# Down projection of a hybrid decoder layer: 8 of 22 feature blocks of each half as two Strassen steps of seven products, with a plain tile behind each unit

## The chip, the cores and the metric

The kernel runs on one core of a Trainium2 chip, in one launch. The metric is the device time of one execution in microseconds (us). Three executions of the kernel before took 1077.84, 1078.82 and 1079.95 us; their median is 1078.82 us. The profile is of one further execution, which took 1077.04 us.

## The reference, cut to what matters

One decoder layer on 256 tokens (S) and a model width of 2048 (D). The matrices are float32.

```python
h = rmsnorm(x, attn_norm_g)
proj = h @ w_in                       # one combined input projection
o_mla = mla_group(...)                # 8 heads, latent queries and keys
o_nsa = nsa_group(...)                # 16 heads, three branches
x = x + concatenate([o_mla, o_nsa]) @ w_o
h = rmsnorm(x, ffn_norm_g)
x = x + (silu(h @ w_gate) * (h @ w_up)) @ w_down     # D_FF = 5632
return rmsnorm(x, final_norm_g)
```

The change is about the product with `w_down`, a matrix of 5632 x 2048. Its left factor has 256 rows (the tokens) and 5632 columns (the features), which are 44 blocks of 128.

## The kernel before

The layer is worked through in stages: input projection, attention, output projection, and the feed-forward part. The feed-forward part runs in two halves of 22 feature blocks each (NFH = 22). A half first computes the gate and up projections of its 22 blocks, then adds its share of the down projection to `x`. So the order of the long stages is gate and up of half 0, down of half 0, gate and up of half 1, down of half 1, and a short tail with the final norm and the output.

All weights come through one class, `Stream`. The order of the tiles is the list that `program()` returns (from L81 on for this part). A weight tile is 128 x 1024 float32, 512 KB, and is loaded by a DMA that SyncE issues (L122). ScalarE then makes the high part by a cast to the reduced type fp32r (`whi`, L143), and VectorE the low part by subtracting the high part from the raw tile (`wlo`, L145). Each of the three tags (`wraw`, `whi`, `wlo`) has three buffers. A load is issued up to three tiles ahead (DMA_AHEAD, L104), and a split is recorded two tiles ahead (SPLIT_AHEAD, L105). The activations are kept in a high and a low part as well (`aT`), and every product is the sum of three matmuls: high by high, high by low and low by high (L859 to L861).

The down projection of a half goes through four groups of 512 output columns (`dg`, L844), and in each group through 11 tiles of two feature blocks (L864). A tile makes 12 matmuls of 128x128 by 128x512: two halves of the tokens (t), two blocks, three matmuls each. The sums of a group stand in two PSUM banks; behind the 11 tiles VectorE adds them to `x` (L876). In half 1, ScalarE also sums the squares (L880) and GpSimd multiplies by the final gain `gfin` (L882). In the last group the matmuls of four tiles for the second half of the tokens are held back to the end (`held`, L867), and the last tiles' parts have buffers of their own (`W.apart`, L812). The gain is loaded ahead of the gate and up projections, on GpSimd's queue (L811).

The order of TensorE's instructions is the order in which the code records them. The order on the other engines is set by a scheduler from its own model of their times. At the very start, the input projection's first two tiles (880 columns) are each loaded and split in two pieces, cut at column 368 (L111).

Of the kernel before, what the change touches and what calls it, by code (L numbers as in the profile page):

```python
# [9 lines left out]
F32 = mybir.dt.float32  # L10
# [6 lines left out]
P = 128  # L17
# [13 lines left out]
NSA_SCALE = 0.125  # L31


def program():
# [46 lines left out]
    for h in range(2):  # L81
# [6 lines left out]
        s += [("w", ("down", h, dg, j)) for dg in range(4) for j in range(NFH // 2)]  # L88
    return s


def plan():

    return [k[1] for k in program() if k[0] == "w"]
# [6 lines left out]
class Stream:  # L101
# [3 lines left out]
    SPLIT_AHEAD = 2  # L105

    def __init__(self, nc, pool, order, src):
        self.nc, self.pool, self.order, self.src = nc, pool, order, src
        self.raw, self.done = {}, {}
        self.nd = self.ns = self.nu = 0  # L110
        self.cuts = {0: (0, 368, G1W), 1: (0, 368, G1W)}  # L111
        self.apart = {}
        self.share = 0

    def _dma(self, upto):
        while self.nd < min(upto, len(self.order)):
            i = self.nd
            w = width(self.order[i])
            t = self.pool.tile([P, 1024], F32, tag="wraw", name=f"wraw{i}", bufs=self.DMA_AHEAD)
# [3 lines left out]
            self.raw[i] = t  # L123
            self.nd += 1

    def _split(self, upto):
        nc = self.nc
        while self.ns < min(upto, len(self.order)):
            i = self.ns
            self._dma(i + 1)  # L130
            raw = self.raw.pop(i)
            if self.order[i][0] in ("w1k", "w1v"):
                self.done[i] = raw
            else:
                w = width(self.order[i])
                if i in self.apart:
                    hi, lo = (self.apart[i].tile([P, 1024], F32R, name=f"w{n}{i}") for n in ("hi", "lo"))
                else:
                    hi, lo = (self.pool.tile([P, 1024], F32R, tag=f"w{n}", name=f"w{n}{i}", bufs=3)
                              for n in ("hi", "lo"))  # L140
                cut = self.cuts.get(i, (0, w))
# [9 lines left out]
    def get(self, key):  # L151
        i = self.nu
        assert self.order[i] == key, (self.order[i], key)
# [7 lines left out]
def layer_kernel(ctx: ExitStack, tc: tile.TileContext, a: dict, out: bass.AP):  # L161
# [9 lines left out]
    W = Stream(nc, wp, order, wsrc)  # L171
# [22 lines left out]
    oT = cp.tile([P, 16, 2, S], F32R, name="oT")  # L194
# [35 lines left out]
    ap = att.enter_context(tc.tile_pool(name="att", bufs=1))  # L230

# [553 lines left out]
    def gate_up(key, w):  # L785
        n, f, j = key
        hi, lo = w
        if j == 0:
            st[n, f] = bank("ds" if n == "gate" else "PT", f"{n}{f}")
# [19 lines left out]
    aT = fp.tile([P, NFH, 2, S], F32R, name="aT")  # L809
# [4 lines left out]
    def next_weights(*key):  # L814
        assert next(steps) == ("w", key)
        return W.get(key)

    def activate(h, f):

        t2 = fp.tile([P, 2, S], F32, tag="t2", name=f"t2_{h}_{f}", bufs=2)  # L820
        u = fp.tile([P, 2, S], F32, tag="gu", name=f"u_{h}_{f}", bufs=2)
# [7 lines left out]
        nc.vector.tensor_mul(u[:, 1, :], sl, u[:, 1, :])  # L829
        split(aT[:, f, 0, :], aT[:, f, 1, :], u[:, 1, :])  # L830

    for h in range(2):
# [11 lines left out]
        for dg in range(4):  # L844
            if dg % 2 == 0:
                dn = bank2(f"dn{h}_{dg}")
                pts = [dn[:, 0, :], dn[:, 1, :]]
            else:
                pts = [bank("S0", f"dn{h}_{dg}_0"), bank("O", f"dn{h}_{dg}_1")]
            last = h == 1 and dg == 3  # L850
            ntile = NFH // 2

            def down(t, j, w):
                hi, lo = w
# [16 lines left out]
            for t in range(2):  # L871
                if t == 1:
                    for j, w in held:
                        down(1, j, w)
# [148 lines left out]
```

## Time and profile before

| | us |
|---|---|
| three runs | 1077.84, 1078.82, 1079.95 |
| the profiled execution | 1077.04 |
| its span | 1075.3 |
| gate and up, from the last part of half 0 to its end | to 581.2 |
| down projection of half 0 | 581.2 to 700.8 |
| gate and up of half 1 | 700.8 to 946 |
| down projection of half 1 | 946.1 to 1066.9 |
| tail | 1066.9 to 1075.3 |

The span is the stretch between the first and the last instruction that the profiler saw; the execution's own time is 1.74 us more. PE is the matrix engine and PEld its weight loads, DVE is VectorE, ACT is ScalarE, POOL is GpSimd, and SP is SyncE, which issues the loads. A matmul's row is longer than the distance to the next one, since they are pipelined. In a row of the timeline the bracket at the end says how long the engine was idle before the row, and what it was released by. Durations of single matmuls, casts and subtracts are read from the groups by line; the distance of two instructions from their starts.

### The profile page before, as it was taken

The numbers are of one execution on the slowest core, as the hardware profiler recorded it, in microseconds if no ns is written. First come the engines' busy times: TensorE is split into PE (matmuls) and PEld (weight loads), VectorE is DVE, ScalarE is ACT, GpSimd is POOL, SyncE is SP. The second block draws the span as 40 slices with busy tenths as digits, with TensorE's granted clock in tenths as the row PEclk, the third lists the DMA queues.
The fourth block names the chain that finished last, engine by engine and source line by source line (L and its number), as shares of the span: only waits on it lengthen the run. The fifth ranks groups of instructions, "written<-read, shape, count | busy, mean of one in ns | idle before, by whom it ended". The sixth has DMA issues, their size and how long they took to land.

```text
span 1075.3 us, 16205 instructions
## 1 busy us (share of the span) xinstructions
PE 1052.0 (98%) x6102; PEld 920.3 (86%) x6102; DVE 645.7 (60%) x1017; ACT 562.9 (52%) x994; POOL 205.5 (19%) x207
## 2 busy tenths in 40 slices
PE   8999998999999999999999999999999999999996
PEld 7999997888888888888888888888888888888885
DVE  5668889885656555555555444455555555555554
ACT  5748887854455544545444333345445454444442
POOL 2235445533342101011010000001010110101110
PEclk9999999999999999999999999999999999999998
DMA  8845433334456555555555555555556565666653
GB/s 291 277 145 177 134 119 99 103 100 152 135 178 215 183 190 195 183 190 191 185 192 189 192 191 194 193 196 186 188 194 187 186 194 185 191 194 195 192 191 128
DMA packets 54831, 193.57 MB, mean 180 GB/s; under 512 B 6436, under 2 KB 6948, under 8 KB 54624
## 3 DMA queue, kind: packets, MB, share of 16 engines
q1 hardware_dynamic: 54288, 191.36, 54.7%
q8 instruction: 48, 0.79, 0.3%
q0 software_dynamic: 464, 1.17, 0.3%
q14 instruction: 31, 0.25, 0.1%
HBM read 190.41 MB, written 2.10 MB: 179 GB/s over the span
## 4 chain that ended last, share of the span: by engine, by line
PE 88%; DVE 4%; DMA 4%; ACT 2%; issue 1%; SPq 0%; POOL 0%; DVEq 0%; POOLq 0%; ACTq 0%
PE up L794 15%; PE gate L794 15%; PE up L797 8%; PE gate L797 8%; PE dn L860 7%; PE dn L861 7%; PE dn L859 7%; DMA wraw<-in_g_dram 2%; PE ps_q L214 1%; PE woM L743 1%; PE woM L745 1%; PE woM L744 1%; PE ps_q L215 1%; PE ps_q L216 1%; DVE wlo L145 1%
## 5 line engine op out<-in xcount | busy, mean ns | idle before, releaser
L145 DVE TENSOR_TENSOR wlo<-wraw,whi 128x1024 fp32r<-128x1024 f32 (+3 forms) x352 | 417.6, 1187 | 381.0 <-ACT whi L143 379.7
L143 ACT CAST whi<-wraw 128x1024 fp32r<-128x1024 f32 (+2 forms) x352 | 366.4, 1041 | 441.5 <-PE dn L861 127.9
L794 PE MATMUL gate<-h2T,whi 128*128 128x512 f32 x704 | 221.2, 396 | 0.0
L794 PE MATMUL up<-h2T,whi 128*128 128x512 f32 x704 | 221.1, 395 | 0.0
L827 POOL TENSOR_TENSOR u<-t,RB 128x512 f32<-128x512 f32 x44 | 57.2, 1300 | 553.9 <-DVE t L826 553.9
L797 PEld LDWEIGHTS up<-h2T,wlo 128*128 128x128 f32 x704 | 132.2, 188 | 31.3
L797 PEld LDWEIGHTS gate<-h2T,wlo 128*128 128x128 f32 x704 | 132.2, 188 | 31.2
L797 PE MATMUL gate<-h2T,wlo 128*128 128x256 f32 x704 | 138.3, 278 | 0.0
L797 PE MATMUL up<-h2T,wlo 128*128 128x256 f32 x704 | 138.3, 278 | 0.0
L860 PE MATMUL dn<-wlo,aT 128*128 128x512 f32 x352 | 137.1, 389 | 0.6 <-DVE wlo L145 0.6
L859 PE MATMUL dn<-whi,aT 128*128 128x512 f32 x352 | 136.9, 389 | 0.0
L861 PE MATMUL dn<-whi,aT 128*128 128x512 f32 x352 | 136.9, 389 | 0.0
L147 POOL TENSOR_TENSOR wlo<-wraw,whi 128x256 fp32r<-128x256 f32 x70 | 88.5, 1265 | 139.6 <-ACT whi L143 121.1
L794 PEld LDWEIGHTS gate<-h2T,whi 128*128 128x128 f32 x704 | 107.3, 189 | 0.2
L794 PEld LDWEIGHTS up<-h2T,whi 128*128 128x128 f32 x704 | 107.2, 189 | 0.0
L860 PEld LDWEIGHTS dn<-wlo,aT 128*128 128x128 f32 x352 | 66.1, 188 | 14.7 <-DVE wlo L145 1.0
L859 PEld LDWEIGHTS dn<-whi,aT 128*128 128x128 f32 x352 | 66.1, 188 | 13.8
L861 PEld LDWEIGHTS dn<-whi,aT 128*128 128x128 f32 x352 | 66.1, 188 | 13.5
L214 PE MATMUL ps_q<-hT,whi 128*128 128x256 f32 x128 | 37.4, 292 | 1.6 <-ACT RB L210 1.6
L216 PE MATMUL ps_q<-hT,wlo 128*128 128x256 f32 x128 | 36.2, 283 | 0.0
L215 PE MATMUL ps_q<-hT,whi 128*128 128x256 f32 x128 | 36.2, 283 | 0.0
L743 PE MATMUL woN<-whi,oT 128*128 128x512 f32 x64 | 26.6, 416 | 0.4 <-ACT oT L547 0.4
(323 smaller groups left out, 1486.6 us busy)
## 6 DMA issues: line engine op xcount, KB each, us to landing
wraw<-in_w_dram SPq DMA_DIRECT2D x338, 512.0 KB, 3.5
wraw<-in_g_dram SPq DMA_DIRECT2D x14, 440.0 KB, 5.0
x<-in_x_dram SPq DMA_DIRECT2D x4, 512.0 KB, 6.8
out_dram<-x SPq DMA_DIRECT2D x8, 256.0 KB, 2.6
xt<-in_xT_dram SPq DMA_DIRECT2D x3, 512.0 KB, 5.0
gfin<-in_gfin_dram POOLq DMA_DIRECT2D x1, 1024.0 KB, 6.0
wraw<-in_g_dram SPq DMA_DIRECT2D x2, 256.0 KB, 4.1
wraw<-in_g_dram SPq DMA_DIRECT2D x2, 184.0 KB, 3.3
```

The source lines that it names most:

```text
L143: nc.scalar.copy(hi[:, c0:c1], raw[:, c0:c1])
L145: nc.vector.tensor_sub(lo[:, c0:c2], raw[:, c0:c2], hi[:, c0:c2].bitcast(F32))
L147: nc.gpsimd.tensor_sub(lo[:, c2:c1], raw[:, c2:c1], hi[:, c2:c1].bitcast(F32))
L214: nc.tensor.matmul(ps, hi, act[:, 0, :], start=start, stop=False)
L215: nc.tensor.matmul(ps, hi, act[:, 1, :], start=False, stop=False)
L216: nc.tensor.matmul(ps, lo, act[:, 0, :], start=False, stop=stop)
L794: nc.tensor.matmul(pt, hi[:, kk * P:(kk + 1) * P], h2T[:, k], start=k == 0, stop=False)
L797: nc.tensor.matmul(pt[:, 0:S], lo[:, kk * P:(kk + 1) * P], h2T[:, k, 0, :], start=False, stop=k == KD - 1)
L827: nc.gpsimd.tensor_mul(u, t2, RB[:, None, :].to_broadcast([P, 2, S]))
L859: nc.tensor.matmul(pts[t], h_, wh, start=f == 0, stop=False)
L860: nc.tensor.matmul(pts[t], h_, wl, start=False, stop=False)
L861: nc.tensor.matmul(pts[t], l_, wh, start=False, stop=f == NFH - 1)
```

## The change

Take a 2 x 2 block product: the left factor has the blocks A11, A12 (first half of the tokens; first and second feature block) and A21, A22 (second half), the weights B11, B12 (first feature block; first and second group of columns) and B21, B22. Done plainly it is eight block products. In the form of Strassen and Winograd it is seven, with sums of the blocks ahead and sums of the results behind. The change does the first 8 of the 22 feature blocks of each half in this way.

- *Passes, steps and units.* The four groups of columns become two passes of two groups (`p`). A pass has two steps (NS) of four feature blocks; a step has seven units, in the order B11, P1, P3, P2, B22, P4, B21. Each unit is one tile of weights and one product of 6 matmuls. Behind the first six units of step 0 and the first five of step 1 stands a plain tile (12 matmuls); three plain tiles follow at the end. A pass thus has 14 units, 11 + 3 plain tiles, and 22 loads.
- *Sums of weights.* P1 = B11 + B12, P3 = B12 + B22, P2 = P1 + B22 and P4 = P2 + B21 are made by VectorE, in raw float32, from raw tiles; the split follows as for any tile. They take buffers of the tag `wraw`, three of them. A unit's sums are recorded up to four units ahead (SUM_AHEAD), its split two ahead as before.
- *Raw tiles.* From the first down projection on the raw tiles have six buffers of their own (`raw`), and loads run up to six ahead. A buffer is free when the sums and the split that read it are done.
- *Activations.* For the 8 blocks, seven forms of each pair of blocks are kept in two parts (`aS`): A11, A12, A22 and four sums S1 to S4, made by VectorE in `activate` behind every second block of a pair. The other 14 blocks stay as they were (`aN`).
- *Results.* The products and the plain tiles add up in eight PSUM banks per pass. Behind the last product, `combine()` makes the sums: one copy on ScalarE, four operations on VectorE, and four additions to `x` on GpSimd. VectorE adds the four banks of the plain tiles to `x` at the end of the pass.
- *Around it.* The final gain is loaded when the second down projection is recorded, into a buffer of the attention part that is free by then. The second tile of the input projection is loaded and split in one piece. The buffers of `W.apart` are gone, and three tiles are held back in the last pass in place of four. In half 1 gate's banks alternate between the tags S0 and O.

```diff
+NS = 2
+UNITS = ("B11", "P1", "P3", "P2", "B22", "P4", "B21")
+LOADS = {"B11": (0, 0), "P1": (0, 1), "P3": (1, 1), "P4": (1, 0)}
+SUMS = {"P1": ("B11", "B12"), "P3": ("B12", "B22"), "P2": ("P1", "B22"), "P4": ("P2", "B21")}
+RAW_OF = {"B11": "B11", "P1": "B12", "P3": "B22", "P4": "B21"}
+PLAIN = (2, 4), (3, 8)
+PRODUCT = {"B11": (A11, 1), "P1": (S1, 5), "P3": (S3, 7), "P2": (S2, 6), "B22": (S4, 3), "P4": (A22, 4), "B21": (A12, 2)}
+def down_units(h, p):
+    plain = [("w", ("down", h, 2 * p + c, j)) for j in range(2 * NS, NFH // 2) for c in range(2)]
+    s = []
+    for i in range(NS):
+        for u in UNITS:
+            s.append(("sw", u, h, p, i))
+            if u in UNITS[:6 if i < NS - 1 else 5]:
+                s.append(plain.pop(0))
+    return s + plain
...
-        s += [("w", ("down", h, dg, j)) for dg in range(4) for j in range(NFH // 2)]
+        s += [u for p in range(2) for u in down_units(h, p)]
...
     DMA_AHEAD = 3
     SPLIT_AHEAD = 2
+    SUM_AHEAD = 4
...
-        self.cuts = {0: (0, 368, G1W), 1: (0, 368, G1W)}
-        self.apart = {}
+        self.cuts = {0: (0, 368, G1W)}
+        self.raws = (pool, "wraw", 3)
...
+    def _sum(self, upto):
+        while self.na < min(upto, len(self.units)):
+            u = self.units[self.na]
+            if u[0] != "sw":
+                self.parts[self.na] = self._take()
+            else:
+                what, at = u[1], u[2:]
+                if what in RAW_OF:
+                    r = RAW_OF[what]
+                    self.parts[at, r, "i"], self.parts[at, r] = self._take()
+                if what in SUMS:
+                    x, y = (self.parts[at, n] for n in SUMS[what])
+                    t = self.parts[at, what] = self.pool.tile([P, 1024], F32, tag="wraw", name=f"{what}_{self.na}", bufs=3)
+                    self.nc.vector.tensor_add(t, x, y)
+                    if what == "P3":
+                        self._spent(at, "B12")
+                self.parts[self.na] = None, self.parts[at, what]
+            self.na += 1
...
-        self._dma(i + self.DMA_AHEAD)
+        self._dma(self.nr + self.DMA_AHEAD)
+        self._sum(i + (self.SUM_AHEAD if unit[0] == "sw" else self.SPLIT_AHEAD))
         self._split(i + self.SPLIT_AHEAD)
...
-    gfin = fp.tile([P, D], F32, name="gfin")
-    nc.gpsimd.dma_start(gfin, a["gfin"])
-    W.apart = {len(order) - 2: fp, len(order) - 1: fp}
+    aN = fp.tile([P, NN, 2, S], F32R, name="aN")
+    aS = fp.tile([P, NS, 2, 2, 7, P], F32R, name="aS")
+    W.raws = (fp, "raw", 6)
...
+        nc.vector.tensor_sub(s1, a22, a21)
+        nc.vector.tensor_sub(s3, a11, a21)
+        nc.vector.tensor_add(s2, a11, s1)
+        nc.vector.tensor_sub(s4, a12, s2)
...
+        W.DMA_AHEAD = 6
+        if h == 1:
+            gfin = hp.tile([P, D], F32, tag="big", name="gfin")
+            nc.gpsimd.dma_start(gfin, a["gfin"])
+        for p in range(2):
...
+            def combine():
+                e, u, v, w = (temp(f"e{n}_{h}{p}") for n in range(4))
+                nc.scalar.copy(e, m[1])
+                nc.gpsimd.tensor_add(x11, x11, e)
+                nc.vector.tensor_sub(u, e, m[6])
+                nc.vector.tensor_add(w, u, m[5])
+                nc.gpsimd.tensor_sub(x12, x12, w)
+                nc.vector.tensor_add(u, u, m[7])
+                nc.vector.tensor_add(v, u, m[5])
+                nc.gpsimd.tensor_add(x21, x21, u)
+                nc.gpsimd.tensor_sub(x22, x22, v)
...
+            for n, unit in enumerate(todo):
+                w = W.get(unit[1] if unit[0] == "w" else unit)
+                if unit[0] == "sw":
+                    form, to = PRODUCT[unit[1]]
+                    i = unit[4]
+                    mms(to, w, lambda k: [aS[:, i, k, b, form, :] for b in range(2)])
+                    if unit[1] == "B21" and i == NS - 1:
+                        combine()
+                    continue
+                plain(0, unit[1], w)
+                if end and n >= len(todo) - 3:
+                    held.append((unit[1], w))
                 else:
-                    down(1, j, w)
+                    plain(1, unit[1], w)
```

VectorE's row in the down projection of half 0 before, around the end of the first group of columns; the first number in a name counts the tiles of the program.

```order
L145 TENSOR_TENSOR wlo187_6616<-wraw187_6595,whi187_6615 128x1024
L145 TENSOR_TENSOR wlo188_6634<-wraw188_6613,whi188_6633 128x1024
L145 TENSOR_TENSOR wlo189_6652<-wraw189_6631,whi189_6651 128x1024
L145 TENSOR_TENSOR wlo190_6674<-wraw190_6649,whi190_6673 128x1024
L876 TENSOR_TENSOR x_69<-x_69,dn0_0_6468 128x512
L876 TENSOR_TENSOR x_69<-x_69,dn0_0_6468 128x512
L145 TENSOR_TENSOR wlo191_6692<-wraw191_6671,whi191_6691 128x1024
```

VectorE's row now, in the first pass of half 0, from the end of its first step into its second. A number behind `wlo`, `P1`, `P2`, `P3` or `P4` counts units, one behind `wraw` counts loads. `P1_193` is the first sum of the second step; `wlo188` is the low part of the first step's P4, and `wlo192` that of the plain tile behind the second step's B11.

```order
L197 TENSOR_TENSOR P1_193_6699<-wraw188_6633,wraw190_6637 128x1024
L223 TENSOR_TENSOR wlo188_6654<-P4_188_6639,whi188_6653 128x1024
L223 TENSOR_TENSOR wlo189_6670<-wraw187_6561,whi189_6669 128x1024
L223 TENSOR_TENSOR wlo190_6680<-wraw186_6559,whi190_6679 128x1024
L223 TENSOR_TENSOR wlo191_6702<-wraw188_6633,whi191_6701 128x1024
L197 TENSOR_TENSOR P3_195_6741<-wraw190_6637,wraw192_6695 128x1024
L197 TENSOR_TENSOR P2_197_6773<-P1_193_6699,wraw192_6695 128x1024
L223 TENSOR_TENSOR wlo192_6714<-wraw189_6635,whi192_6713 128x1024
L223 TENSOR_TENSOR wlo193_6726<-P1_193_6699,whi193_6725 128x1024
```

Between the subtracts there are now sums, and a sum stands ahead of subtracts of earlier units: P1 of the second step (which reads load 190) ahead of the low part of P4, and P3 and P2 (which read load 192) ahead of the low part of unit 192.

SyncE's row at the same place, with what each load waits for: the load that last filled the buffer (DMAHW, one of eight counters taken in turn), and VectorE, which reads it last. Before:

```order
L122 DMA wraw184_6541<-in_w_dram 128x1024 [waits DMAHW4_49,DVE_49]
L122 DMA wraw185_6559<-in_w_dram 128x1024 [waits DMAHW5_49,DVE_49]
L122 DMA wraw186_6577<-in_w_dram 128x1024 [waits DMAHW6_49,DVE_49]
L122 DMA wraw187_6595<-in_w_dram 128x1024 [waits DMAHW7_49,DVE_49]
L122 DMA wraw188_6613<-in_w_dram 128x1024 [waits DMAHW0_49,DVE_49]
```

And now:

```order
L167 DMA wraw188_6633<-in_w_dram 128x1024 [waits DMAHW5_49,DVE_49]
L167 DMA wraw189_6635<-in_w_dram 128x1024 [waits DMAHW6_49,DVE_49]
L167 DMA wraw190_6637<-in_w_dram 128x1024 [waits DMAHW4_49,DVE_49]
L167 DMA wraw191_6651<-in_w_dram 128x1024 [waits DMAHW7_49,DVE_49]
L167 DMA wraw192_6695<-in_w_dram 128x1024 [waits DMAHW1_49,DVE_49]
```

Before, the buffers go round in turn. Now they do not: load 190 takes the buffer of load 182 (B22 of the first step, whose low part is unit 186), and load 192 that of load 187 (the plain tile whose low part is unit 189).

## Rows read from the trace of the kernel before

**Rows 1.** Busy time, share of the span and instructions of each engine.
```profile
PE 1052.0 (98%) x6102; PEld 920.3 (86%) x6102; DVE 645.7 (60%) x1017; ACT 562.9 (52%) x994; POOL 205.5 (19%) x207
```

**Rows 2.** The chain that ended last, by engine and by line.
```profile
PE 88%; DVE 4%; DMA 4%; ACT 2%; issue 1%; SPq 0%; POOL 0%; DVEq 0%; POOLq 0%; ACTq 0%
PE up L794 15%; PE gate L794 15%; PE up L797 8%; PE gate L797 8%; PE dn L860 7%; PE dn L861 7%; PE dn L859 7%; DMA wraw<-in_g_dram 2%; PE ps_q L214 1%; PE woM L743 1%; PE woM L745 1%; PE woM L744 1%; PE ps_q L215 1%; PE ps_q L216 1%; DVE wlo L145 1%
```

**Rows 3.** Windows: length, busy PE PEld DVE ACT POOL, PEclk, DMA share, GB/s.
```profile
581.19:700.78 119.59, 119.59 (x530) 99.04 (x529) 58.60 (x54) 47.40 (x47) 1.30 (x1) 1.00 0.59 194
700.80:946.00 245.20, 245.20 (x1410) 213.91 (x1409) 140.09 (x175) 119.19 (x173) 27.25 (x21) 1.00 0.59 189
946.10:1066.90 120.80, 120.15 (x530) 98.83 (x528) 60.60 (x58) 50.31 (x60) 10.94 (x8) 1.00 0.56 180
```

**Rows 4.** Down half 0 by line: durations min/median/max ns, first and last start.
```profile
L859 PE MATMUL dn<-whi,aT x176: 389/389/395, 581.2 to 700.2; 128*128 128x512 f32 x176
L876 DVE TENSOR_TENSOR x<-x,dn x7: 680/680/689, 611.3 to 700.6; 128x512 f32<-128x512 f32 x7
...
L145 DVE TENSOR_TENSOR wlo<-wraw,whi x44: 1218/1225/1226, 582.3 to 699.4; 128x1024 fp32r<-128x1024 f32 x44
```

**Rows 5.** Timeline, one tile: start, duration, what [idle before, releaser].
```profile
583.92 0.39 PE L859 MATMUL dn<-whi,aT 128*128 128x512 f32 x1
...
584.12 1.06 ACT L143 CAST whi<-wraw 128x1024 fp32r<-128x1024 f32 x1 [1.60 <-PE dn L861]
...
585.21 1.22 DVE L145 TENSOR_TENSOR wlo<-wraw,whi 128x1024 fp32r<-128x1024 f32 x1 [1.36 <-ACT whi L143]
```

**Rows 6.** Timeline near the end of half 1's down projection.
```profile
1054.85 2.36 DVE L145 TENSOR_TENSOR wlo<-wraw,whi 128x1024 fp32r<-128x1024 f32 x2 [2.87 <-ACT whi L143]
...
1056.27 0.39 PE L859 MATMUL dn<-whi,aT 128*128 128x512 f32 x1
...
1057.26 0.50 PE L860 MATMUL dn<-wlo,aT 128*128 128x512 f32 x1 [0.61 <-DVE wlo L145]
```

**Rows 7.** Loads, 581.1 to 700.9, then 800 to 1010; last, median us to landing.
```profile
wraw<-in_w_dram SPq DMA_DIRECT2D x44, 512.0 KB, 3.4
...
wraw<-in_w_dram SPq DMA_DIRECT2D x76, 512.0 KB, 4.3
```

**Rows 8.** Timeline in half 1's down projection, GpSimd beside VectorE.
```profile
977.98 3.06 POOL L882 TENSOR_TENSOR x<-x,gfin 128x512 f32<-128x512 f32 x2 [27.78 <-ACT fsq L880]
...
980.08 2.05 DVE L145 TENSOR_TENSOR wlo<-wraw,whi 128x1024 fp32r<-128x1024 f32 x1 [1.43 <-ACT whi L143]
```

**Rows 9.** GpSimd's product in `activate` by line, durations min/median/max ns.
```profile
L827 POOL TENSOR_TENSOR u<-t,RB x44: 1293/1298/1410, 355.4 to 948.9; 128x512 f32<-128x512 f32 x44
```

**Rows 10.** Loads issued from 337 to 339, then from 339.5 to 341.
```profile
gfin<-in_gfin_dram POOLq DMA_DIRECT2D x1, 1024.0 KB, 6.0
...
wraw<-in_w_dram SPq DMA_DIRECT2D x1, 512.0 KB, 4.9
```

**Rows 11.** Timeline of the start, the input projection's second and third tile.
```profile
8.28 0.62 ACT L143 CAST whi<-wraw 128x512 fp32r<-128x512 f32 x1 [0.55 <-DMA wraw<-in_g_dram]
...
9.17 0.28 PE L216 MATMUL ps_kc<-hT,wlo 128*128 128x256 f32 x1
...
10.12 0.93 ACT L143 CAST whi<-wraw 128x880 fp32r<-128x880 f32 x1 [0.24 <-DMA wraw<-in_g_dram]
...
12.21 0.39 PE L216 MATMUL ps_kc<-hT,wlo 128*128 128x256 f32 x1 [0.41 <-DVE wlo L145]
```

**Rows 12.** Windows with a lower granted clock, and one with idle time of PE.
```profile
68.00:70.00 2.00, 2.00 (x18) 2.00 (x17) 0.83 (x1) 1.14 (x2) 0.79 (x1) 0.92 0.47 125
70.00:72.00 2.00, 2.00 (x10) 1.82 (x10) 1.30 (x4) 0.00 (x0) 0.71 (x1) 0.50 0.48 170
72.00:74.00 2.00, 2.00 (x15) 2.00 (x14) 0.00 (x0) 0.00 (x0) 0.00 (x0) 0.72 0.94 313
192.00:200.00 8.00, 7.43 (x60) 6.85 (x59) 7.42 (x17) 7.63 (x21) 5.51 (x7) 1.00 0.23 78
```

More of the change, by code (lines that the diff above doesn't have):

```diff
@@ L87, in program, with loads @@
                 s += w(*A("gate", f), *A("up", f))
-        s += [("w", ("down", h, dg, j)) for dg in range(4) for j in range(NFH // 2)]
+        s += [u for p in range(2) for u in down_units(h, p)]
     return s
+def loads(step):
+    if step[0] == "w":
+        return [step[1]]
+    if step[0] == "sw" and step[1] in LOADS:
+        u, h, p, i = step[1:]
+        r, c = LOADS[u]
+        return [("down", h, 2 * p + c, 2 * i + r)]
+    return []
 def plan():
-    return [k[1] for k in program() if k[0] == "w"]
+    return [k for s in program() for k in loads(s)]
 def width(key):
@@ L126, in _split @@
     def _split(self, upto):
         nc = self.nc
[L128 to L132, printed above, removed]
+        while self.ns < min(upto, len(self.units)):
+            i, u = self.ns, self.units[self.ns]
+            self._sum(i + 1)
+            n, raw = self.parts.pop(i)
+            if u[0] != "sw":
+                self.live.discard(n)
+            elif u[1] in ("B11", "B22", "B21"):
+                self._spent(u[2:], u[1])
+            if u[0] in ("w1k", "w1v"):
@@ L133, in _split @@
                 self.done[i] = raw
             else:
[L135 to L141, printed above, removed]
+                w = width(u) if u[0] != "sw" else 1024
@@ new lines, in mms, with plain @@
+                    h_, l_ = left(k)
+                    nc.tensor.matmul(m[to], h_, wh, start=first and k == 0, stop=False)
+                    nc.tensor.matmul(m[to], h_, wl, start=False, stop=False)
+                    nc.tensor.matmul(m[to], l_, wh, start=False, stop=last and k == 1)
+            def plain(t, key, w):
+                f = 2 * key[3] - 4 * NS
+                mms(PLAIN[key[2] % 2][t], w, lambda k: [aN[:, f + k, b, t * P:(t + 1) * P] for b in range(2)])
+            def combine():
[9 more added lines that the diff above has]
+                nc.gpsimd.tensor_sub(x22, x22, v)
@@ new lines, in layer_kernel @@
+            end = h == 1 and p == 1
+            held = []
+            for n, unit in enumerate(todo):
+                assert next(steps) == unit
+                w = W.get(unit[1] if unit[0] == "w" else unit)
[9 more added lines that the diff above has]
+                    held.append((unit[1], w))
+                else:
+                    plain(1, unit[1], w)
@@ new lines, in layer_kernel @@
+            if not end:
+                for xs, b in ((x11, 2), (x21, 4), (x12, 3), (x22, 8)):
+                    nc.vector.tensor_add(xs, xs, m[b])
+                if h == 1:
+                    for t in range(2):
+                        final(t, (2 * p, 2 * p + 1))
+                continue
+            nc.vector.tensor_add(x11, x11, m[2])
+            nc.vector.tensor_add(x12, x12, m[3])
+            final(0, (2 * p, 2 * p + 1))
+            for b in range(2):
+                for key, w in held:
+                    if key[2] % 2 == b:
+                        plain(1, key, w)
+                nc.vector.tensor_add((x21, x22)[b], (x21, x22)[b], m[4 if b == 0 else 8])
+                final(1, (2 * p + b,))
```

149 lines of the change are left out of this document (86 added, 63 removed).

## Prediction

> **What bounds the kernel now.** I read the page's totals first. The span is 1075.3 us and PE is busy 98% of it [rows 1]. A matmul's row is longer than its pitch, though, so a busy PE says only that something is always in flight. The chain that ended last is 88% PE, with gate and up matmuls at its head and 21% for the down projection [rows 2]. Then the stretches: the down projection of half 0 takes 119.59 us and that of half 1 takes 120.80 us, with DVE busy for 58.60 and 60.60 us of them, ACT for 47.40 and 50.31 [rows 3]. So PE sets the pace there, and DVE has about half of the time free.
>
> The pitch comes from the down rows. L859 is one of three matmul lines that take turns; it has 176 instructions in half 0, the first at 581.2 and the last at 700.2, so matmuls stand (700.2 - 581.2) / (175 x 3) = 0.227 us apart, though each reads 389 ns [rows 4]. A matmul removed is worth 0.227 us, not 0.389. A plain tile is 12 matmuls, 2.72 us; a product is 6, 1.36 us.
>
> The path from a free buffer to a usable tile comes next. The first matmul of a new tile starts at 583.92, which is when PE leaves the tile before. ACT's cast, released by that, starts at 584.12, 0.20 later, and takes 1.06. DVE's subtract starts at 585.21 and takes 1.22 [rows 5]. From PE's release to a ready low part that is 2.5 us. Two subtracts back to back take 2.36, so the second costs only 1.14 [rows 6]. A load lands 3.4 us after its issue in half 0, but 4.3 from 800 to 1010 [rows 7].
>
> **The change part by part.** *Matmuls.* Each half has two passes (pairs of column groups), each pass two steps, each step seven products of 6 matmuls in place of eight. That is 2 x 2 x 2 x 6 = 48 matmuls fewer, 48 x 0.227 = **-10.9 us**.
>
> *The stall at the end of half 1.* PE's matmul at 1056.27 is followed by the next one at 1057.26, 0.99 later in place of 0.23, because the last tiles' loads were late. That one reads 0.50 in place of 0.39: a restart costs 0.11 more [rows 6]. Six raw buffers issue these loads earlier: **-0.9** (0 to -0.9).
>
> *DVE's load.* A pass has 28 units of work in place of 22 tiles, 14 x 2.72 + 14 x 1.36 = 57.1 us of PE. DVE has 28 subtracts of 1.14 to 1.22 (32 to 34 us), and 8 weight sums. No row shows a sum. The nearest is the subtract of the same size, 1.22 [rows 4], so 9.8 us. A different output type could make it cheaper or dearer: the 512-wide add from PSUM takes 0.68 [rows 4], two of these make 1.36, and nothing shows under 1.14. Four combining operations and four adds at 0.68 are 5.4. Together 47 to 50 of 57 us, about 85%: it fits on the average, and order decides. ACT has 28 x 1.06 = 30 us and stays clear. The extra forms of the activations fall into the gate and up stretch, where DVE is busy 140 of 245 us [rows 3]: four sums of 128 columns and wider splits for every second of eight blocks per half, under 3 us in 22 us. I cost them at 0; the cover is one tile of PE time.
>
> *The sums in DVE's row.* This is the first place that I think stalls. Take the unit list of a pass with the ninth unit as B22. Let PE release the sixth unit (a plain tile) at 0. The low part of B22 is ready at 2.5. Only now is B22's raw buffer free, and the load of the next step's B12 (190 in the listing) goes out at 2.5 and lands at 6.0. DVE's row has the sum P1 of the next step ahead of the subtract of P4 (the eleventh unit), so P1 ends at 7.2 and the low part of P4 at 8.3. PE meanwhile runs 1.36 + 2.72 + 1.36 + 2.72 = 8.16 and wants this low part for its second matmul at 8.39. The slack is 0, the cost 0 to 0.2.
>
> The second place follows directly. The subtract of the plain tile behind P4 ends at 9.5. It frees the buffer for the next step's B22 (192), which lands at 13.0. P3 and P2 stand ahead of the subtract of the plain tile behind the next B11: 1.22 + 1.14 + 1.14 after 13.0 is 16.5. PE gets there after the eleventh to fourteenth units, 1.36 + 2.72 + 1.36 + 1.36, and one matmul more: 8.4 + 6.8 + 0.2 = 15.4. It waits 1.1. With 0.1 at the first place and 0.11 for each restart that is 1.4 per pass, **+5.7** for four. The lower end is 0: if the sums cost nothing, or a load lands a us sooner, the wait is gone. The upper end is the landing of 4.3 below.
>
> *From pass to pass.* Behind the last products come three plain tiles, 8.2 us. DVE has the combining (2.7), three or four subtracts and the next pass's first three sums; POOL adds to x four times. What POOL does to DVE is seen at 980.08: a subtract beside POOL's multiply takes 2.05 in place of 1.22, with POOL running from 977.98 for 3.06, so 0.96 us of overlap cost 0.83 [rows 8]. Four POOL operations of 1.3 [rows 9] could take 4.5 us from DVE. PE wants the second tile of the next pass about 11.1 us after the release from which its sum's load starts, and I get 11.1 for its low part without POOL. So 0 to 1.5 at each of the two boundaries; I take 0.6: **+1.2**. The Trainium skill, "SBUF — State Buffer", section "Who interferes with whom", says that a DVE operation with two SBUF inputs and a POOL operation that reads SBUF exclude each other for a whole instruction. By that, four times 1.3 would come out of DVE here, 5.2 in place of 4.5; the trace's 0.83 of 0.96 is close to it.
>
> *Loads.* The stretch of slow landings covers a fifth of the span and would meet some pass. From 3.4 to 4.3 adds 0.9 at the first place and 0.9 at the second; a whole half costs some 5 us more. I take **+1.5** (0 to 10). The gains' load now starts with the second down projection. Before, it took 6.0 and a load beside it 4.9, 1.5 more than 3.4 [rows 10]: 0 to 1.5, I take **+0.5**.
>
> *The start.* The second input tile comes whole. Its second piece was there for ACT at 8.28, and PE took the first low part of that tile at 9.17 [rows 11]. Now a whole cast, 0.93 for 880 columns [rows 11], and a subtract, 1.22 x 880 / 1024 = 1.05, start at 8.28 and end at 10.26. That is 1.1 late; the 0.41 that PE is idle ahead of 12.21 for the next tile [rows 11] goes. **+0.7** (-0.4 to 1.1). The last products after the final matmul keep their chain; I cost them at 0 (within 0.2).
>
> **Sum.** -10.9 - 0.9 + 5.7 + 1.2 + 1.5 + 0.5 + 0.7 = -1.2. The profiled execution took 1077.04 us, 1.74 beyond its span of 1075.3, so it would take 1075.8; the median of the three runs, 1078.82, lies 1.8 above the profiled one. **Forecast 1077.6 us**, less than can be told: 0.2%, 2.2 us, is about what a measurement of this kernel tells from no change.
>
> **Rivals.** *All hidden.* Landings at 3.0, or sums under 1.1, leave no wait: -11.8 + 1.2, **1068**. For it: DVE's 15% of free time. Against it: the walk, in which a load waits for a subtract and a subtract for that load's sums.
>
> *Slower: the ring of raw buffers.* With landings at 4.3 everywhere the first place waits 1.0, the second 2.1, the boundary 1.9, and the start of each half 0.9: 4 x 3.3 (with two restarts) + 2 x 1.9 + 2 x 0.9 = 18.8, against 11.8 saved and 1.2 of small costs: +8, **1087**. It decides from where the waits make 10.6: they grow by about 13 us for each us of landing, from 7 at 3.4, so from a mean landing of 3.7. For it: the trace has 4.3 for 210 us [rows 7], and bursts of loads share engines. Against it: half 0 shows 3.4 throughout.
>
> *No change.* Landings of 3.5 to 3.8, or POOL taking all of 4.5: **1079**.
>
> *The clock falls.* Ten PE waits of 1 to 2 us could lose PE its clock, 2.4 GHz at a granted 1.00. Around 70 it read 0.92, 0.50 and 0.72 in three stretches of 2 us [rows 12], which costs 2 x (0.08 + 0.50 + 0.28) = 1.7; eight falls like that make +14, **1091**. Against it: at 192 to 200 PE was idle for 0.57 us and the clock stayed at 1.00, while it fell at 68 to 72 with PE busy throughout [rows 12]. The Trainium skill, "TensorE: Matmul & The Clock Gate", section "HAM oscillation — how this bites in real kernels", has the clock fall after waits for DMA; these rows don't show waits doing it.
>
> **How the numbers follow.** Forecast case 0.45 (own range 1073 to 1081), all hidden 0.17, landings and buffers 0.20, no change 0.14, clock 0.04. Faster by over 0.2%: not quite half of the forecast case (0.21) and all of "hidden", with a little of "no change" (0.02), 0.40. Within 0.2%: 0.20 and 0.12, 0.32. Slower: the ring, the clock and 0.04 of the forecast case, 0.28. The range runs from "hidden" to the ring's price: 1068 to 1087.
>
> **What would show it.** The down rows at a 0.227 pitch and 1008 of them; PE waiting for DVE's low part just behind the second step's B11 in every pass, 1 to 2 us, and hardly anywhere else; DVE there waiting for a load. Wrong would be: waits at every product (DVE is too slow, not too late), waits for ACT, no waits at all, or a clock below 1.00 in the passes.

## The result, and the profile after

The changed kernel takes 1086.8 us (median of four runs, 1086.16 to 1088.96). Against the kernel before the ratio is 1.0089, interval 1.0072 to 1.0105: it is slower by 0.9%, where the forecast was 1077.6 us, a little faster. By the two medians, 1086.8 and 1078.82, it is 0.7%; a fourth execution of the kernel before took 1492.92 us and counts in neither figure. The profiled execution took 1086.16 us. Its page gives the span, the busy times, and the chain that ended last:

```profile
span 1084.4 us, 16294 instructions
...
PE 1047.1 (97%) x6054; PEld 910.1 (84%) x6054; DVE 742.7 (68%) x1126; ACT 594.7 (55%) x1031; POOL 237.2 (22%) x221
...
PE 76%; DVE 11%; DMA 6%; issue 3%; ACT 3%; SPq 0%; POOL 0%; DVEq 0%; POOLq 0%; ACTq 0%
PE gate L875 15%; PE up L875 15%; PE gate L878 8%; PE up L878 7%; DVE wlo L223 6%; DMA wraw<-in_w_dram 5%; PE m L992 3%; PE m L993 2%; PE m L991 2%; ACT whi L221 1%; PE ps_q L292 1%; PE ps_q L293 1%; PE ps_q L294 1%; PE woM L823 1%; PE woM L824 1%
```

PE has the 48 matmuls less (6054 against 6102, [rows 1]). But its share of the chain fell from 88% to 76% [rows 2]. What came in is VectorE's subtract (6%) and the weight loads (5%). The windows of the two down projections, with gate and up of half 1 between them, in the columns of [rows 3]:

```profile
581.70:702.70 121.00, 116.90 (x506) 93.77 (x505) 98.13 (x88) 60.87 (x61) 17.52 (x9) 1.00 0.58 190
702.80:947.90 245.10, 245.10 (x1409) 213.85 (x1408) 148.88 (x198) 120.88 (x177) 27.25 (x21) 1.00 0.58 190
948.00:1075.90 127.90, 117.86 (x506) 93.42 (x504) 100.72 (x90) 64.48 (x75) 26.29 (x15) 1.00 0.49 160
```

All of the loss but 0.6 us stands in the down projections; the clock is at 1.00 in both. The down projections from the start of their first matmul to the start of their last one, and the two ends, before and after (us):

| stretch | before | after | difference |
|---|---|---|---|
| start to the first gate matmul | 334.9 | 335.4 | +0.5 |
| down, half 0 | 119.5 | 120.8 | +1.4 |
| down, half 1 | 120.4 | 127.5 | +7.1 |
| from the last matmul to the end | 8.8 | 8.9 | +0.1 |

That is the 9.1 us by which the span grew; the gate and up projections between take the same in both kernels. In half 0 before, without waits, 527 distances between matmuls make 119.5 us, 0.2267 each, so the 504 matmuls of a half would now take 503 x 0.2267 = 114.0. The rest is 6.8 us in half 0 and 13.5 in half 1. The distances that are clearly longer than the others, each less 0.227, show where 6.5 and 13.0 of it are; this is called lost time from here on. PE's waits of half 0 (581 on) and of half 1, from the view of waits (us in total, times, longest), all have one releaser, VectorE's low part:

```profile
PE m L992 <- DVE wlo L223: 4.1, 6, 1.1
...
PE m L992 <- DVE wlo L223: 9.9, 9, 3.5
```

By place, from the same distances:

| place | us lost | foreseen |
|---|---|---|
| plain tile behind the second step's B11, four passes | 1.21, 1.25, 1.01, 1.04 | 1.1 each |
| first of the last three plain tiles, directly behind the last product B21 | 0.72, 0.74, 0.70, 0.69 | none |
| second step's P3 | 0.45, 0.14 (half 0), 1.39 (half 1, first pass) | none |
| start of the second pass | 0.69 (half 0), 0.96 + 0.35 + 1.57 (half 1) | 0.6 each |
| first step's P3, half 1 | 3.63 | 0.5 (the gain) |
| restarts (0.11 each), first step's P4 (0.1 to 0.3) and others | about 3 | 0.1 each |

The first of these places, in the timeline of the first pass (start, duration, what, idle before):

```profile
607.08 1.23 DVE L197 TENSOR_TENSOR P<-wraw,wraw 128x1024 f32<-128x1024 f32 x1 [0.82 <-DMA wraw<-in_w_dram]
...
608.22 1.22 DVE L197 TENSOR_TENSOR P<-P,wraw 128x1024 f32<-128x1024 f32 x1
...
609.35 1.22 DVE L223 TENSOR_TENSOR wlo<-wraw,whi 128x1024 fp32r<-128x1024 f32 x1
...
610.63 0.50 PE L992 MATMUL m<-wlo,aN 128*128 128x512 f32 x1 [1.05 <-DVE wlo L223]
```

This is the walk of the prediction: a load that comes late, two sums behind it, then the subtract that PE is waiting for. A sum takes 1.22, as the prediction took it from [rows 4]. The same chain stands where the prediction did not look, at the second step's P3, here in half 1: the sum P4 (first row) waits for its load, the subtract of P3 (second row) stands behind it, and PE waits for that.

```profile
986.38 1.23 DVE L197 TENSOR_TENSOR P<-P,wraw 128x1024 f32<-128x1024 f32 x1 [2.58 <-DMA wraw<-in_w_dram]
...
987.53 1.22 DVE L223 TENSOR_TENSOR wlo<-P,whi 128x1024 fp32r<-128x1024 f32 x1
...
988.80 0.50 PE L992 MATMUL m<-wlo,aS 128*128 128x512 f32 x1 [1.23 <-DVE wlo L223]
```

The worst place is the start of half 1's down projection:

```profile
953.37 1.03 ACT L221 CAST whi<-P 128x1024 fp32r<-128x1024 f32 x1
957.26 1.23 DVE L197 TENSOR_TENSOR P<-P,wraw 128x1024 f32<-128x1024 f32 x1 [5.39 <-DMA wraw<-in_w_dram]
...
958.73 1.22 DVE L223 TENSOR_TENSOR wlo<-P,whi 128x1024 fp32r<-128x1024 f32 x1
...
960.01 0.50 PE L992 MATMUL m<-wlo,aS 128*128 128x512 f32 x1 [3.47 <-DVE wlo L223]
```

ScalarE had the high part of P3 ready at 954.4. VectorE stood idle for 5.39 us all the same, because the sum P4 is next in its row and waits for the load of B21; the subtract of P3, which needs nothing any more, is behind it. That load took 8.8 us, while the gain was loaded (issues from 948 to 949, then two rows of those from 948 to 960; KB each, median us to landing); e1 below shows that the gain's load is the reason.

```profile
wraw<-in_w_dram SPq DMA_DIRECT2D x1, 512.0 KB, 8.8
...
wraw<-in_w_dram SPq DMA_DIRECT2D x2, 512.0 KB, 7.7
gfin<-in_gfin_dram POOLq DMA_DIRECT2D x1, 1024.0 KB, 8.9
```

And the end of a pass, where VectorE combines and GpSimd adds to `x`:

```profile
627.54 1.82 DVE L223 TENSOR_TENSOR wlo<-P,whi 128x1024 fp32r<-128x1024 f32 x1
...
628.24 2.27 POOL L1008 TENSOR_TENSOR x<-x,e 128x512 f32<-128x512 f32 x1
629.28 0.67 DVE L1007 TENSOR_TENSOR e<-e,m 128x512 f32<-128x512 f32 x1
...
630.48 2.27 POOL L1009 TENSOR_TENSOR x<-x,e 128x512 f32<-128x512 f32 x1
...
633.89 0.50 PE L992 MATMUL m<-wlo,aN 128*128 128x512 f32 x1 [0.56 <-DVE wlo L223]
```

Beside GpSimd a subtract takes 1.82 and not 1.22, and GpSimd's own operations 2.27 and not 1.3 [rows 9]; its first addition here, at 626.98, took 1.29.

### The profile page after: what moved, and what is told of

It reads as the page before. It is cut to its first block, busy times and chain, and to the rows that moved or that the text cites. A ratio compares the mean times of both kernels' runs of the same rounds, so it can differ in the third digit from the quotient of the medians.

```text
span 1084.4 us, 16294 instructions
## 1 busy us (share of the span) xinstructions
PE 1047.1 (97%) x6054; PEld 910.1 (84%) x6054; DVE 742.7 (68%) x1126; ACT 594.7 (55%) x1031; POOL 237.2 (22%) x221
## 4 chain that ended last, share of the span: by engine, by line
PE 76%; DVE 11%; DMA 6%; issue 3%; ACT 3%; SPq 0%; POOL 0%; DVEq 0%; POOLq 0%; ACTq 0%
PE gate L875 15%; PE up L875 15%; PE gate L878 8%; PE up L878 7%; DVE wlo L223 6%; DMA wraw<-in_w_dram 5%; PE m L992 3%; PE m L993 2%; PE m L991 2%; ACT whi L221 1%; PE ps_q L292 1%; PE ps_q L293 1%; PE ps_q L294 1%; PE woM L823 1%; PE woM L824 1%
## 5 line engine op out<-in xcount | busy, mean ns | idle before, releaser
L221 ACT CAST whi<-wraw 128x1024 fp32r<-128x1024 f32 (+2 forms) x343 | 357.8, 1043 | 371.4 <-PE gate L875 77.6
L992 PE MATMUL m<-wlo,aN 128*128 128x512 f32 x224 | 88.6, 396 | 7.6 <-DVE wlo L223 7.6
L993 PE MATMUL m<-whi,aN 128*128 128x512 f32 x224 | 87.3, 390 | 0.0
L991 PE MATMUL m<-whi,aN 128*128 128x512 f32 x224 | 87.3, 390 | 0.0
L992 PEld LDWEIGHTS m<-wlo,aN 128*128 128x128 f32 x224 | 42.0, 188 | 21.0 <-DVE wlo L223 12.6
L221 ACT CAST whi<-P 128x1024 fp32r<-128x1024 f32 x32 | 33.7, 1052 | 43.8 <-PE m L993 40.3
L992 PE MATMUL m<-wlo,aS 128*128 128x512 f32 x112 | 44.7, 399 | 6.5 <-DVE wlo L223 6.4
L991 PEld LDWEIGHTS m<-whi,aN 128*128 128x128 f32 x224 | 42.1, 188 | 9.0
L993 PEld LDWEIGHTS m<-whi,aN 128*128 128x128 f32 x224 | 42.1, 188 | 8.4
L223 DVE TENSOR_TENSOR wlo<-P,whi 128x1024 fp32r<-128x1024 f32 x32 | 42.6, 1330 | 2.9 <-ACT whi L221 2.9
L993 PE MATMUL m<-whi,aS 128*128 128x512 f32 x112 | 43.7, 390 | 0.0
```

Source lines behind the costliest of these rows:

```text
L221: nc.scalar.copy(hi[:, c0:c1], raw[:, c0:c1])
L223: nc.vector.tensor_sub(lo[:, c0:c2], raw[:, c0:c2], hi[:, c0:c2].bitcast(F32))
L991: nc.tensor.matmul(m[to], h_, wh, start=first and k == 0, stop=False)
L992: nc.tensor.matmul(m[to], h_, wl, start=False, stop=False)
L993: nc.tensor.matmul(m[to], l_, wh, start=False, stop=last and k == 1)
```

## The experiments

Each ratio is against the kernel before, in runs on the same chip. The changed kernel was not run again beside the experiments, so a difference to it is one of medians from different sessions. Lost time is PE's, per half, half 0 first, worked out as above; it is read from the traces and is finer than the whole times, since the start of the first gate matmul alone varies from 334.6 to 338.7 between these runs, over code that is the same in them (but for e11).

**e1: the gain loaded early.**

```diff
+    gfin = fp.tile([P, D], F32, name="gfin")
+    nc.gpsimd.dma_start(gfin, a["gfin"])
     for h in range(2):
...
-            gfin = hp.tile([P, D], F32, tag="big", name="gfin")
-            nc.gpsimd.dma_start(gfin, a["gfin"])
```

> The changed kernel with the final gain loaded ahead of the gate and up projections again, into a buffer of its own, as in the kernel before. Theory A (the 8.9 us load of the gain delays the weight loads of half 1's down projection): the wait of 3.6 us at the second product P3 of half 1's first pass goes, with some of the waits that follow it in that pass; down half 1 shrinks by 3.5 to 5 us, to about 1083 in all. Theory B (VectorE has too much to do, whatever the loads do): the wait moves to a later product and the time stays within 1 us of 1086.8.

1081.93 us, ratio 1.0045 (1.003 to 1.006). The wait of 3.63 is gone, and half 1 loses 8.7 in place of 13.0, 4.3 less. Theory A held. Most of the rest stayed.

**e2: nine raw buffers.**

```diff
-    W.raws = (fp, "raw", 6)
+    W.raws = (fp, "raw", 9)
...
-        W.DMA_AHEAD = 6
+        W.DMA_AHEAD = 9
```

> The changed kernel with nine raw buffers and loads up to nine ahead in place of six. Theory A (a load waits for a buffer that a late subtract frees, and the sums wait for that load): the four waits of 1.0 to 1.25 at the plain tile behind the second step's B11, those at P3 of the second step and those at the start of a second pass go, about 9 us, and the gain's load is partly covered too: about 1076 to 1079. Theory B (VectorE has too much to do): the waits stay, 1085 to 1087.

1087.14 us, ratio 1.0099 (1.0074 to 1.0123): no gain; lost: 7.9 and 9.9. The waits at the plain tile behind the second B11, at the second step's P3 and at the gain's load are gone, and half 0's at the start of the second pass, as A had it. But with loads further ahead the scheduler also put two sums of the next pass ahead of the last three subtracts of this one. The timeline of the first pass's end:

```profile
634.29 1.72 DVE L197 TENSOR_TENSOR P<-wraw,wraw 128x1024 f32<-128x1024 f32 x1
...
635.93 2.28 DVE L197 TENSOR_TENSOR P<-P,wraw 128x1024 f32<-128x1024 f32 x1
638.13 3.48 DVE L223 TENSOR_TENSOR wlo<-wraw,whi 128x1024 fp32r<-128x1024 f32 x3
639.40 0.79 PE L992 MATMUL m<-wlo,aN 128*128 128x512 f32 x1 [3.78 <-DVE wlo L223]
```

These sums wait for no load, and still PE waits 3.8 us at the end of each first pass (beside GpSimd the two take 4.0 in place of 2.4). So neither theory was enough: the sums' place in the row costs, with a late load or without one. What late loads alone cost in the old order is not separated by this run, since it changed both.

**e3: no additions by GpSimd.** The four lines `nc.gpsimd.tensor_add(x11, x11, e)` to `nc.gpsimd.tensor_sub(x22, x22, v)` are left out.

> The changed kernel without the four additions to x by GpSimd in the combining step (left out of the computation). Theory A (GpSimd stretches VectorE's subtracts beside it, 2.3 and 1.8 us in place of 1.2): the wait of 0.7 us at the last tile but one of every pass goes, 2.8 to 3.3 us in all, and 1 to 2 us of the waits at the start of the second passes: about 1082. Theory B (these waits come from late loads): no change there, 1086 to 1087.

1084.44 us, ratio 1.0062 (1.0041 to 1.0083), between the two theories' times; lost: 5.2 and 12.0. The place called the last tile but one there is the one behind the last product; all four waits of 0.7 are gone, and no subtract of half 0 takes over 1.23. So these come from GpSimd beside VectorE. The waits at the second pass hardly changed (0.57, and 1.12 + 0.36 + 1.60), and P3's grew in half 0 to 1.00: part of what one place gives back is lost at the next.

**e4: no sums.** The buffer of B12 is then free once P3 is split, not once it is summed.

```diff
-                    x, y = (self.parts[at, n] for n in SUMS[what])
-                    t = self.parts[at, what] = self.pool.tile([P, 1024], F32, tag="wraw", name=f"{what}_{self.na}", bufs=3)
-                    self.nc.vector.tensor_add(t, x, y)
-                    if what == "P3":
-                        self._spent(at, "B12")
+                    self.parts[at, what] = self.parts[at, {"P1": "B12", "P3": "B12", "P2": "B22", "P4": "B21"}[what]]
...
```

> The changed kernel with the four sums of weights in each step left out; the units P1 and P3 take the raw tile B12, P2 takes B22 and P4 takes B21 (so these products are not the reference's). VectorE has 32 sums of 1.2 us less and no subtract stands behind a sum that waits for a load. Theory A (order: sums that wait for loads block subtracts): all waits but the gain's and those from GpSimd go, some 10 us: 1075 to 1078. Theory B (the products need tiles faster than any load or cast can come): waits remain at the products, over 1082.

1070.49 us, ratio 0.9941 (0.9926 to 0.9955): 16 us less than the changed kernel. Lost: 1.7 and 2.2 us, most of it behind the last product. Even the gain's load, which is still at the start of half 1, costs PE nothing. That was below the expected range: all but what is left behind the last product hangs on the sums. The run takes away both their place in the row and their time, 32 x 1.22 = 39 us of VectorE; e5 tells the two apart.

**e5: the sums held behind earlier subtracts.** A rule of issue order alone, without a wait, and with six raw buffers.

```diff
-                    self.nc.vector.tensor_add(t, x, y)
+                    with self.tc.issue_after(self.behind):
+                        self.nc.vector.tensor_add(t, x, y)
...
-                    nc.vector.tensor_sub(lo[:, c0:c2], raw[:, c0:c2], hi[:, c0:c2].bitcast(F32))
+                    self.behind = nc.vector.tensor_sub(lo[:, c0:c2], raw[:, c0:c2], hi[:, c0:c2].bitcast(F32)).ins
```

> The changed kernel (six raw buffers) with one ordering rule: a sum of weights is put behind the last subtract that was recorded before it in VectorE's row, so it can't stand ahead of subtracts of earlier units. Theory A (a sum that waits for its load, or takes 1.2 us at the wrong moment, holds up subtracts that PE wants sooner): the waits at P3 of the second step and at the plain tile behind the second step's B11 go, and so do those at the start of the second passes; 5 to 9 us less, 1078 to 1082. Theory B (where two products follow each other PE leaves only 2.72 us for a path of 2.5 from a free buffer to a low part, whatever the order): the waits at the plain tile behind the second B11 and at the last tile but one of a pass stay at 0.7 to 1.2 each, over 1083.

1074.91 us, ratio 0.9977 (0.9963 to 0.9991): 12 us less than the changed kernel with the same work, loads and buffers, and now faster than before. Lost: 2.3 and 5.4 us. At the start of half 1, where VectorE had been idle for 5.39 us, the gain is still loaded at the same point. P3's subtract (the first row) now comes as soon as its high part is there, ahead of P2's sum (the second row), and P4's comes later still:

```profile
949.92 1.74 DVE L225 TENSOR_TENSOR wlo<-P,whi 128x1024 fp32r<-128x1024 f32 x1 [0.49 <-ACT whi L223]
...
951.59 1.22 DVE L199 TENSOR_TENSOR P<-P,wraw 128x1024 f32<-128x1024 f32 x1
...
953.06 1.22 DVE L225 TENSOR_TENSOR wlo<-wraw,whi 128x1024 fp32r<-128x1024 f32 x1
```

VectorE has no wait for a load here, and PE none in this pass until the second step. In half 0 the loads now land in a median of 3.5 us, against 3.9 in the changed kernel (issues from 581 to 702.7 there, from 581 to 700 here):

```profile
wraw<-in_w_dram SPq DMA_DIRECT2D x44, 512.0 KB, 3.9
...
wraw<-in_w_dram SPq DMA_DIRECT2D x45, 512.0 KB, 3.5
```

Theory A went further than its range. Of B's places the one behind the second B11 has no wait left (0.3 stands one plain tile later, behind P1), and the one behind the last product keeps 0.5 of 0.7. The largest wait left is 1.7, at the start of half 1's second pass.

**e6: the same rule with nine raw buffers.** The edits of e5 and e2.

> The same ordering rule together with nine raw buffers. Theory A: the waits of 3.9 us that nine buffers alone brought at the end of a first pass came from two sums of the next pass that were put ahead of the last subtracts; they go, and the late loads are covered too: waits of some 2 us in half 0 and 4 in half 1 (the gain's load), 1070 to 1074. Theory B: 0.7 to 1.2 stays at eight places, 1076 to 1080.

1074.77 us, ratio 0.9977 (0.9965 to 0.9988). Lost: 2.3 and 5.4, the same at each place to 0.02 us as in e5. The expectation of 1070 to 1074 was missed: with the sums in this order three more raw buffers change nothing.

**e7: a fourth buffer for the high and low parts,** the order left to the scheduler.

```diff
-                hi = self.pool.tile([P, 1024], F32R, tag="whi", name=f"whi{i}", bufs=3)
-                lo = self.pool.tile([P, 1024], F32R, tag="wlo", name=f"wlo{i}", bufs=3)
+                p4 = self.fourth is not None and i % 4 == 3
+                pool, bufs = (self.fourth, 1) if p4 else (self.pool, 3)
+                hi = pool.tile([P, 1024], F32R, tag="whi", name=f"whi{i}", bufs=bufs)
+                lo = pool.tile([P, 1024], F32R, tag="wlo", name=f"wlo{i}", bufs=bufs)
...
+    W.fourth = fp
```

> The changed kernel with a fourth buffer for the high and the low parts in the down projections (order of the sums left to the scheduler). Theory A (order of the sums and late loads): the waits at P3 and at the start of the second passes stay, a gain of less than 4 us, 1083 or more. Theory B (no slack where two products follow each other): the eight waits at the plain tile behind the second B11 and at the last tile but one of a pass go, 6 to 8 us, 1079 to 1081.

1073.33 us, ratio 0.9961 (0.9946 to 0.9976). Lost: 2.4 and 3.5 us. More than either theory gave, and neither had the places right: 0.6 to 0.8 stays behind the second B11, the waits behind the last product are gone, and so are those at the second step's P3 and the 3.63 at the start of half 1. A tile more of room is 1.4 to 2.7 us of PE's time. But the fourth buffer also moved sums in the row, so whether the room hides the cost of the order, or the order changed, is not told apart here.

**e8: order, fourth buffer and early gain together** (six temporary tiles in place of eight, for room).

> The changed kernel with the ordering rule, the fourth buffer of the parts, and the gain loaded early (six raw buffers, six in place of eight temporary tiles for room). If A and B both hold, each for its own places, hardly any wait is left: the down stages take 114.5 to 116 us each and the whole 1067 to 1070. If VectorE is simply too busy with its sums and GpSimd beside it, waits of over 4 us stay in each half: 1075 or more.

1067.43 us, ratio 0.9906 (0.9891 to 0.9921), as expected. Half 0 loses nothing: it takes 114.0 us from the first matmul to the last. Half 1 loses 1.5, at one place at the start of its second pass:

```profile
1003.00 6.09 POOL L943 TENSOR_TENSOR x<-x,gfin 128x512 f32<-128x512 f32 x3 [2.94 <-ACT fsq L941]
...
1003.39 2.32 DVE L228 TENSOR_TENSOR wlo<-P,whi 128x1024 fp32r<-128x1024 f32 x1
...
1005.63 2.31 DVE L200 TENSOR_TENSOR P<-P,wraw 128x1024 f32<-128x1024 f32 x1
1007.87 2.30 DVE L228 TENSOR_TENSOR wlo<-wraw,whi 128x1024 fp32r<-128x1024 f32 x1
...
1010.22 0.50 PE L996 MATMUL m<-wlo,aN 128*128 128x512 f32 x1 [1.25 <-DVE wlo L228]
```

Three products with the gain run for 6.09 us on GpSimd, and three operations of VectorE in a row take 2.3 each in place of 1.22.

**e9, e10, e11: GpSimd's work on VectorE.** e10 is e8 with the products with the gain on VectorE (`nc.vector.tensor_mul(xs, xs, gfin[...])`); e9 moves the four additions of the combining step as well; e11 is e10 with the second input tile cut in two again.

> The version of e8 with GpSimd's work in the down projections moved to VectorE: the four additions of the combining step and the products with the gain. Theory A (GpSimd and VectorE take turns, so an operation beside GpSimd takes 2.3 us in place of 1.2, and VectorE is better off doing four operations of 0.68 itself): the wait of 1.4 us in half 1's second pass goes and none comes, 1065.5 to 1067. Theory B (VectorE, with some 90% of a pass filled, has no room for more): waits of 0.5 to 2 us come back near the end of each pass, 1068 to 1072.

> The version of e8 with only the products with the gain on VectorE (the additions of the combining step stay on GpSimd). Theory A: the wait of 1.4 us in half 1's second pass, when three of these products run beside VectorE for 6 us, goes; no other wait comes, since the four parts' buffers cover the combining; 1066. Theory B (that wait comes from the many operations at the start of the second pass, not from GpSimd): it stays within 0.3 us, 1067.4.

> The version of e10 with the second input tile loaded and split in two pieces again, as in the kernel before. If the whole tile costs PE a wait at the start, as I reckoned, 0.5 to 0.7 us less than e10. If not, within 0.3 us of it; less than the spread of the runs either way.

e9 1066.07 us, ratio 0.9887 (0.9872 to 0.9901); e10 1066.69, 0.9889 (0.987 to 0.9909); e11 1066.28, 0.9887 (0.9872 to 0.9902). No wait of PE for VectorE is left in any of the three; the down projections of e9 in the columns of [rows 3]:

```profile
583.20:697.40 114.20, 114.20 (x506) 94.64 (x505) 98.81 (x97) 61.14 (x61) 2.27 (x1) 1.00 0.62 203
942.70:1056.90 114.20, 114.20 (x506) 94.43 (x504) 99.07 (x102) 63.38 (x74) 2.82 (x2) 1.00 0.53 167
```

VectorE is busy for 99 us of 114 with GpSimd's work in it, and for 100.6 without (e10, half 0): what it takes over costs it no more than what it lost beside GpSimd. Theory A held in e9 and e10 as to the waits; by their times alone they can't be told from e8 or from each other. The cut of the second tile can't be told from nothing either (e11). All three beat both kernels, by 1.1% and, by the ratios, by 2.0%.

## Why the prediction was wrong

- **The sum: a slip.** The seven terms add up to -2.2 us and not to -1.2, so by its own terms the forecast is 1076.6, off by 10.2 and not by 9.2.
- **Matmuls: right.** 48 x 0.227 = 10.9 us. Without waits each half takes 114.0 us (e10) in place of 119.5 and 120.4, which is 11.8 with the stall of 0.9 at the end of half 1, also as predicted.
- **The sums in DVE's row: the step that failed.** The place that it walked through was right, 1.0 to 1.25 us in every pass against 1.1. But it walked only along the loads 190 and 192, and took every other subtract to come in time. A sum stands ahead of subtracts of earlier units in other places too, and each of them blocks when its load is late: P4 ahead of P3's subtract (2.0 us in the second steps), and the same at the start of half 1 (3.6). The prediction had the chain, "a load waits for a subtract and a subtract for that load's sums", and then followed it to one place only. In all the lost time was 6.5 + 13.0 = 19.5 us, where the terms for sums, borders, loads and the gain added up to 5.7 + 1.2 + 1.5 + 0.5 = 8.9. The 10.6 between them is nearly all of the 11.3 by which the span missed the terms (+9.1 against -2.2). e5 shows the cause: the same work in another order loses 7.7, so 11.8 of the 19.5 hung on the order. GpSimd's places, in the next item, are part of what stays, and what late loads alone would cost in the old order stays open (e2).
- **From pass to pass: right price for GpSimd, wrong place.** GpSimd's four additions cost VectorE 3.3 us in the first pass, within the bound of 4.5: 1.1 in a subtract at 611.63, and at the end of the pass 0.6 in the subtract at 627.54 and 1.6 in the next three, which took 5.09 where 3.5 would do. I let the three plain tiles cover that. But where two products follow each other, PE leaves 2 x 1.36 = 2.72 us for a path of 2.5 [rows 5], and the combining falls just there: 0.7 in every pass (e3). At the second pass of half 1 the products with the gain came on top (e8, e10): 2.9 there, where 0.6 was foreseen.
- **The gain: too small by 3.** I priced the delay of one load (0 to 1.5). The load that P4 waits for was delayed by more (8.8 in place of 3.4), and the sum in front turned that into a wait of PE; without it half 1 lost 4.3 less (e1). In e5 the gain is loaded at the same place and costs nothing there.
- **Loads: the wrong quantity.** Landings of 3.9 in half 0 and 3.8 in half 1 were above the 3.7 from which my slower rival decides, and its time, 1087, is nearly the one measured. That is a coincidence as far as the places go: it has 2.1 at the second place, 1.0 at the first and 0.9 at the start of each half, where 1.0 to 1.25, 0.1 to 0.3, and 0 and 3.6 came. It also has the buffers decide, and e6 with nine of them equals e5 with six; in the old order nine did take the waits away at the walk's places (e2), but moved sums as well. In e5 the loads land in 3.5: part of the slow landing was an effect of the order.
- **ScalarE, the forms of the activations, the tail:** cost nothing to be seen, as predicted; from the last matmul of half 0's down projection to the first of half 1's it is 245.4 in both. The start, +0.5 against +0.7 predicted, can't be told from the spread of the runs.
- **The clock:** 1.00 in both down projections, so that rival did not come in this kernel. It came in e2 and e3 (last section).

## What to carry to other kernels

When an engine gets a second kind of work in its row, list every place where the new instruction stands ahead of an older, ready one, and price each of them by the latest input of the new instruction, not by its duration; an average load of 85% did not show it here. Where a scheduler made the order, try holding the new work behind the old by issue order before adding buffers: it was worth 12 us here, against nothing for three more raw buffers. A fourth buffer for the parts was worth 13 (e7), though the order moved with it; the two together with the early gain were worth 19 (e8). And a helper engine that takes turns with a nearly full one may take no work from it: try the operations on the full engine itself (e9).

## What the runs showed of the hardware that was not expected

A VectorE operation on two operands in SBUF, 1.22 us alone, takes 2.3 with GpSimd busy throughout (e8), while GpSimd's additions go from 1.29 to 2.27 (changed kernel): both engines pay, where [rows 8] had shown me only what VectorE pays. The Trainium skill, "SBUF — State Buffer", section "Who interferes with whom", says that the two engines exclude each other on a shared pair of ports. The trace of e8 is in line with it: 2.31, against 2.52 if the one ran wholly behind the other.

PE's clock can fall after a wait. In e2 PE was idle for 3.78 us, and the stretch behind it was granted 0.60 on the mean, with matmuls 0.43 us apart, so for most of it 1.2 GHz in place of 2.4 (a window of e2, in the columns of [rows 3]):

```profile
639.40:643.00 3.60, 3.60 (x10) 2.89 (x11) 2.21 (x2) 0.00 (x0) 0.00 (x0) 0.60 0.79 193
```

In the changed kernel PE was idle for 3.47 us up to 960, and the stretch behind that stayed at 1.00:

```profile
960.00:964.00 4.00, 3.99 (x17) 3.12 (x18) 3.78 (x4) 2.21 (x3) 0.00 (x0) 1.00 0.35 112
```

The clock also fell in e2's half 1 (0.58), and in e3, where PE was idle nearly throughout from 954.9 to 958.2 and the stretch behind was granted 0.61:

```profile
954.90:958.20 3.30, 0.26 (x2) 0.00 (x0) 2.70 (x4) 1.10 (x2) 0.00 (x0) 1.00 0.02 10
958.20:962.50 4.30, 4.25 (x12) 3.35 (x13) 3.87 (x4) 2.25 (x3) 0.00 (x0) 0.61 0.38 121
```

The Trainium skill, "TensorE: Matmul & The Clock Gate", section "HAM oscillation — how this bites in real kernels", has the clock fall after waits for DMA. The trace of e3 agrees: its wait goes back to the load of B21, for which the sum P4 waited. In e2 the clock fell behind waits that go back to no load, and in the changed kernel it stayed behind one that does. So the clock does fall behind such waits, against what I read from [rows 12], but not behind every one, and what decides is open.
